# Low parts of the weights by an accumulating transfer onto the negated high part, in an encoder trunk with split fp32 products

## The chip, the cores and the metric

The kernel runs on one core of a Trainium2 chip. The metric is the device time of one execution in microseconds (us). Before the change the median of three runs is 3259.91 us (3259.77 to 3260.55).

## What is computed

An encoder trunk of four layers over 512 tokens with 16 learned meta tokens ahead, width 1024, fp32. The mixers of the layers are multi-head latent attention (MLA), differential attention, a bidirectional RG-LRU and MLA again; a SwiGLU feed-forward follows each, and every sub-layer has an RMS norm before and after it. Cut to the frame:

```python
def _swiglu(h, w_in, w_out):
    g, u = jnp.split(h @ w_in, 2, axis=-1)
    return (jax.nn.silu(g) * u) @ w_out
...
def _rglru_block(h, w_in, conv_w, conv_b, w_gates, b_gates, lam, w_o):
    xb, gate = jnp.split(h @ w_in, 2, axis=-1)
    xb = lax.conv_general_dilated(...) + conv_b
    y = (_rg_lru(xb, w_gates[0], ..., reverse=False)
         + _rg_lru(xb, w_gates[1], ..., reverse=True))
    return (y.astype(h.dtype) * jax.nn.gelu(gate)) @ w_o
```

The precision asked for is that of fp32, and TensorE multiplies a rounded form of it, fp32r. So every factor is split in two: `x = xh + xl` and `w = wh + wl`, where the high part is the value rounded to fp32r and the low part is the rest. A product is the sum of three: `wh*xh + wh*xl + wl*xh`.

## The kernel before

Activations are kept transposed, features on the 128 partitions and 528 positions (512 tokens, 16 meta) along the free axis, which a matmul covers in two spans, 272 and 256 wide. The program is eight stages in a row, mixer and feed-forward of each layer, with a `boundary` between two stages (residual, norm, the split of the new `x`, and the first matmuls of the next stage). The order of every instruction on every engine is the order in which the code is written.

All weights lie in HBM in the order of use as 456 chunks of 128 partitions: 344 of 1024 columns, 80 of 768, 16 of 640 and 16 of 512. The class `Weights` hands them out:

- `fetch` (L241) starts a chunk's load into a staging tile `ws` on the queue of SyncE (SP). There are two staging tiles, so a load waits until the split of the chunk two before has read its tile.
- `ensure` (L252) splits chunks in order up to a wanted number. For each, ScalarE (ACT) copies `ws` to `wh` with rounding (L261), and the engine named in `l_engine` subtracts, `wl = ws - wh` (L262). There are four buffers for `wh` and four for `wl`. VectorE (DVE) subtracts 280 chunks, in the feed-forward stages above all, and GpSimd (POOL) 176, in the mixers and the boundaries; `run`, `boundary` and `final` set `l_engine`.
- `next` (L267) hands out the next chunk and first asks `ensure` for the two chunks behind it, so the split of a chunk stands in each engine's order about two chunks ahead of its use. The number that `ensure` may reach is capped by `low`, the oldest chunk still in use, plus the number of buffers.

`mm3` (L340) issues the three products through `mm` (L327). `split_from` (L336) splits an activation: ACT casts the high part and DVE subtracts. In the RG-LRU stage the names are: `t` and `xc` are the convolution's steps on DVE, `xsh` and `xsl` the split of its result, `g` a gate, `th` and `gt` steps of the recurrence, which runs as a scan on DVE (L1532). In MLA a head's query is split into `qh` and `ql`, and its rotary part into `qsa` and `qsb`.

At the start `run` (L1600s) starts the loads of the first three chunks between those of `x`; at the end of the first boundary ACT copies a finished PSUM tile to SBUF (`t<-pa`, L607), which frees the PSUM tile for the next stage.

Of the kernel before, what the change touches and what calls it, by code (L numbers as in the profile page):

```python
# [18 lines left out]
F32 = mybir.dt.float32  # L19
# [6 lines left out]
P = 128  # L26
# [202 lines left out]

class Weights:  # L230

    BUFS = 4

    def __init__(self, k, dram, widths):
        self.k, self.dram, self.widths = k, dram, widths
        self.offs = np.concatenate([[0], np.cumsum(np.array(widths) * P)]).tolist()
        self.n_dma = self.n_split = self.use = self.low = 0
        self.stage, self.parts = {}, {}
        self.l_engine = k.nc.vector

    def fetch(self, upto):  # L241
        while self.n_dma < min(upto + 1, len(self.widths)):
            j = self.n_dma
            n = self.widths[j]
            t = self.k.wpool.tile([P, 1024], F32, name="ws", tag="ws", bufs=2)
            self.k.nc.sync.dma_start(
                out=t[:, 0:n],
                in_=self.dram[self.offs[j]:self.offs[j] + P * n].rearrange("(p n) -> p n", p=P))
            self.stage[j] = t
            self.n_dma += 1  # L250

    def ensure(self, upto):  # L252
        upto = min(upto, self.low + self.BUFS - 1, len(self.widths) - 1)
        while self.n_split <= upto:
            j = self.n_split
            self.fetch(j)
            n = self.widths[j]
            s = self.stage.pop(j)
            wh = self.k.wpool.tile([P, 1024], F32R, name="wh", tag="wh", bufs=self.BUFS)
            wl = self.k.wpool.tile([P, 1024], F32R, name="wl", tag="wl", bufs=self.BUFS)  # L260
            self.k.nc.scalar.copy(out=wh[:, 0:n], in_=s[:, 0:n])  # L261
            self.l_engine.tensor_tensor(out=wl[:, 0:n], in0=s[:, 0:n], in1=f32(wh[:, 0:n]), op=ALU.subtract)  # L262
            self.parts[j] = (wh, wl)
            self.n_split += 1
            self.fetch(j + 2)

    def next(self, hold=False, ahead=2):  # L267
        j = self.use
# [11 lines left out]
class Trunk:  # L280
# [218 lines left out]
    def boundary(self, tail, g1, g2, t0, first=False, last=False, after=None):  # L499

        ha, hb = halves(t0)
        (a0, a1), (b0, b1) = ha, hb
        W = self.W
        todo = [(k, half) for half in (ha, hb) for k in range(NK)]
        running = []

        def adv(n):

            for _ in range(n):
                if todo:
                    k, half = todo.pop(0)
                    running.append([3, self.residual(k, half[0], half[1], g2, first, last)])
                for r in reversed(running):
                    r[0] -= 1
                    next(r[1])
                running[:] = [r for r in running if r[0]]

        def ens(n):  # L520
            if not last:
                W.ensure(W.use + n)

        W.l_engine = self.nc.gpsimd
        if first:
            W.low = W.use
            W.l_engine = self.nc.vector
            ens(0)
            adv(4)
            ens(1)  # L530
            for k in (2, 4, 6):
                self.load_x(k, 1)
            adv(2)
        else:
            stat = {}

            def mid():
                self.tt(self.acc[:, a0:a1], self.acc[:, a0:a1], stat["sq"], ALU.add)
                st = self.stat([self.acc[:, a0:a1]])
                self.rstd(st, self.rpost[:, a0:a1], 1.0 / D)  # L540

            def done():
                W.retire(1)
                ens(3)

            for n, m in enumerate(tail.ms):
                ps = self.ps1()[:, 0:a1 - a0]
                tail(m, ps, a0, a1)
                stat["sq"] = self.evict_u(m, ps, a0, a1, g1, tail.add)
            ens(3)  # L550
            for n, m in enumerate(tail.ms):
                ps = (self.ps1() if n or len(tail.ms) == 1 else self.ps2())[:, 0:b1 - b0]
                early = m == 7 and len(tail.ms) == 2
                tail(m, ps, b0, b1, None if n else mid, (lambda: (adv(3), done())) if early else done)
                adv({5: 1, 6: 2}.get(m, 0) if len(tail.ms) > 2 else 3 * (m == 7 and not early))
                stat["sq"] = self.evict_u(m, ps, b0, b1, g1, tail.add)
            done()
            adv(3)
        parts = {}
        tiles = [] if last else [self.ps2() for _ in range(3)]  # L560

        def group(ks, half):
            if last:
                return
            for k in ks:
                if k // 2 not in parts:
                    parts[k // 2] = W.next(hold=True, ahead=0)
            self.group_half(tiles, parts, ks, *half, col0(t0))

        group(range(2), ha)  # L570
        if last:
            st = self.stat([self.acc[:, b0:b1], stat["sq"]])
            adv(1)
            self.rstd(st, self.rpost[:, b0:b1], 1.0 / D)
            adv(12)
            return None
        if not first:
            st = self.stat([self.acc[:, b0:b1], stat["sq"]])
            rest = self.rstd(st, self.rpost[:, b0:b1], 1.0 / D, late=True)
        if first:  # L580
            ens(1)
        group(range(2, 4), ha)
        adv(2)
        if not first:
            rest()
        ens(0)
        ens(1)
        W.l_engine = self.nc.gpsimd
        adv(2)
        sq = self.sq  # L590
        group(range(4, 8), ha)
        adv(2)
        group(range(0, 2), hb)
        self.tt(self.acc2[:, a0:a1], self.acc2[:, a0:a1], sq, ALU.add, None)
        sa = self.stat([self.acc2[:, a0:a1]])
        rest = self.rstd(sa, self.r[:, a0:a1], 1.0 / D, late=True)
        adv(2)
        group(range(2, 4), hb)
        W.retire(2)
        adv(4)  # L600
        rest()
        W.l_engine = self.nc.vector
        ens(0)
        group(range(4, 8), hb)
        W.retire(2)
        t = self.tmp()
        self.nc.scalar.copy(out=t[:, t0:NT], in_=tiles[0][:, col0(t0) + t0:col0(t0) + NT])  # L607
        tiles[0] = Shifted(t, col0(t0))
        sb = self.stat([self.acc2[:, b0:b1], self.sq])
        self.rstd(sb, self.r[:, b0:b1], 1.0 / D)  # L610
        if after is not None:
            self.load_table(after)
        ens(1)
        return tiles
# [19 lines left out]
    def final(self, get_chunks, kt, g1, t0, split, add=False):  # L634
# [3 lines left out]
        rng = spans(t0)  # L638
        W = self.W
        self.load_table(RSQRT)  # L640
        W.l_engine = self.nc.vector
        lead0 = W.use - len(self.led)
        for m in range(8 - split):
            if m in self.led:
# [14 lines left out]
                W.ensure(W.use + 1)  # L659
            self.evict_u(m, ps[:, col0(t0) + t0:col0(t0) + NT], t0, NT, g1, add)  # L660
        held, first = {}, self.W.use
        W.l_engine = self.nc.gpsimd
        for m in range(8 - split, 8):
            n = self.W.use
            self.W.low = max(self.W.low, min(self.W.use, first))
# [942 lines left out]
    def run(self):  # L1608
        nc, tc = self.nc, self.tc
        make_identity(nc, self.ident)  # L1610
        nc.vector.memset(self.ones, 1.0)
        nc.vector.memset(self.eps, EPS)
        self.load_table(RSQRT)
        nc.scalar.dma_start(out=self.sm[:, 0:S_MLA], in_=self.aps["small"][:, 0:S_MLA])
        for n in range(3):
            self.W.fetch(n)
            self.load_x(2 * n, 0)
        self.load_x(6, 0)
        self.load_x(0, 1)
        nc.scalar.dma_start(out=self.sm[:, S_MLA:S_N], in_=self.aps["small"][:, S_MLA:S_N])  # L1620
        tail, g1 = None, None
        for s in range(STAGES + 1):
            i = s // 2
            g2 = (lambda k, i=i, w=(2 if s % 2 else 0): self.gain(i, w, k)) if s < STAGES else None
            late = s >= 7 or s == STAGES
            t0 = NMETA if late else 0
            after = AF.Silu if s % 2 else (AF.Sigmoid if s == 4 else None)
            tiles = self.boundary(tail, g1, g2, t0, first=(s == 0), last=(s == STAGES), after=after)
            self.close_phase()
            if s == STAGES:  # L1630
                break
            self.open_phase()
            self.W.l_engine = nc.vector if s % 2 else nc.gpsimd
            if s % 2:
                tail, g1 = self.ffn(tiles, i, t0)
            elif s == 2:
                tail, g1 = self.diff(tiles, i)
            elif s == 4:
                tail, g1 = self.lru(tiles, i)
            else:  # L1640
                tail, g1 = self.mla(tiles, i, i // 3, NMETA if s == 6 else 0)
# [34 lines left out]
```

## Time and profile before

| | |
|---|---|
| median of three runs | 3259.91 us |
| the profiled execution | 3257.35 us |
| its span | 3255.3 us |
| granted TensorE clock, mean | 0.979 |
| TensorE (PE) busy | 3065.2 us, 94% |
| VectorE (DVE) busy | 1882.9 us, 58% |
| ScalarE (ACT) busy | 1395.9 us, 43% |
| GpSimd (POOL) busy | 752.7 us, 23% |
| read from HBM | 225.34 MB, 70 GB/s over the span |

The span is the time between the first and the last instruction of the profiled execution; some 2 us of its own time lie outside it. Busy shares are means over stages with different limits, so they are read together with the windows by stage. A wait is put down to the work that came last before it ended. A row of the timeline stands for neighbouring instructions of one kind; its duration is from the first one's start to the last one's end.

### The profile page before, as it was taken

How to read it: one execution, taken by the hardware profiler on the slowest of the kernel's cores; microseconds unless marked ns; L12 is line 12 of the kernel's file. 1: busy time of each engine (PE TensorE's matmuls, PEld its weight loads, DVE VectorE, ACT ScalarE, POOL GpSimd, SP SyncE). 2: the span in 40 equal slices, each digit the busy share in tenths (PEclk: the TensorE clock that was granted, in tenths of full speed). 3: DMA queues.
4: the chain of work that ended last, by engine and by line, in shares of the span. 5: the costliest groups of instructions: out<-in, count | busy, mean ns of one | idle time of the engine just before them, and what ended most of it. 6: DMA issues, size and time to landing. Idle time of an engine off the chain costs nothing. (4 is left out here: it accounts for less than half of the span.)

```text
span 3255.3 us, 53413 instructions
## 1 busy us (share of the span) xinstructions
PE 3065.2 (94%) x22384; PEld 2892.2 (89%) x22384; DVE 1882.9 (58%) x3003; ACT 1395.9 (43%) x2464; POOL 752.7 (23%) x514
## 2 busy tenths in 40 slices
PE   8999999999989998999988889999998999999998
PEld 7898898999979888999977889999987888888887
DVE  7766747443277767443278874544248676574433
ACT  5554544222256565222246553322235554442232
POOL 3232222000145523000045543000033322330001
PEclk9999999999999999999998999999999999999999
DMA  3011112222211112222221212222221111122222
GB/s 102 31 45 48 37 46 78 90 91 92 90 62 40 56 37 72 91 91 93 88 67 59 67 58 90 91 91 89 95 65 55 47 37 48 53 77 96 97 97 80
DMA packets 71600, 230.88 MB, mean 71 GB/s; under 512 B 7824, under 2 KB 12304, under 8 KB 71360
## 3 DMA queue, kind: packets, MB, share of 16 engines
q1 hardware_dynamic: 70144, 225.54, 21.5%
q8 instruction: 176, 2.88, 0.4%
q10 hardware_dynamic: 1216, 1.93, 0.2%
q14 instruction: 64, 0.52, 0.0%
HBM read 225.34 MB, written 2.10 MB: 70 GB/s over the span
## 5 line engine op out<-in xcount | busy, mean ns | idle before, releaser
L327 PE MATMUL pa<-xh,wh 128*128 128x272 f32 (+2 forms) x4120 | 955.0, 303 | 18.3 <-ACT xh L318 7.5
L327 PE MATMUL pa<-xh,wl 128*128 128x272 f32 (+2 forms) x3776 | 891.3, 299 | 3.5 <-POOL wl L262 3.5
L327 PE MATMUL pa<-xl,wh 128*128 128x272 f32 (+1 forms) x3776 | 809.8, 288 | 43.9 <-DVE xl L324 43.2
L327 PEld LDWEIGHTS pa<-xl,wh 128*128 128x128 f32 x3776 | 620.2, 190 | 88.9 <-DVE xl L324 59.3
L327 PEld LDWEIGHTS pa<-xh,wh 128*128 128x128 f32 x4120 | 665.0, 190 | 34.9 <-DVE ql L324 9.1
L262 DVE TENSOR_TENSOR wl<-ws,wh 128x1024 fp32r<-128x1024 f32 (+1 forms) x280 | 330.6, 1183 | 510.3 <-ACT wh L261 510.3
L327 PEld LDWEIGHTS pa<-xh,wl 128*128 128x128 f32 x3776 | 615.6, 190 | 8.6 <-POOL wl L262 3.9
L262 POOL TENSOR_TENSOR wl<-ws,wh 128x1024 fp32r<-128x1024 f32 (+3 forms) x176 | 388.8, 2215 | 725.6 <-ACT wh L261 665.8
L321 POOL TENSOR_TENSOR acc<-acc,t 128x256 f32<-128x256 f32 (+3 forms) x158 | 164.2, 1040 | 1528.2 <-ACT t L318 1523.9
L261 ACT CAST wh<-ws 128x1024 fp32r<-128x1024 f32 (+3 forms) x456 | 440.6, 980 | 160.2 <-DMA ws<-in_w 142.9
L321 DVE TENSOR_TENSOR t<-pa,r 128x528 f32<-128x528 f32 (+1 forms) x193 | 135.5, 703 | 277.5 <-PE pa L327 277.4
L327 PE MATMUL pa<-hh,wl 128*128 128x272 f32 (+2 forms) x1078 | 249.6, 301 | 0.0
L327 PE MATMUL pa<-hl,wh 128*128 128x272 f32 (+2 forms) x1078 | 248.5, 300 | 0.0
L327 PE MATMUL pa<-hh,wh 128*128 128x272 f32 (+2 forms) x1078 | 246.6, 299 | 0.0
L337 ACT CAST hh<-t 128x528 fp32r<-128x528 f32 (+1 forms) x88 | 55.4, 630 | 400.0 <-DVE t L321 400.0
L793 ACT CAST pth<-pa 128x528 fp32r<-128x528 f32 (+3 forms) x200 | 118.7, 593 | 236.7 <-PE pa L782 234.8
L318 ACT ACTIVATE t<-t 128x528 f32<-128x528 f32 (+3 forms) x121 | 72.2, 597 | 294.0 <-DVE t L321 292.7
L327 PEld LDWEIGHTS pa<-hh,wh 128*128 128x128 f32 x1078 | 171.3, 189 | 6.4
L327 PEld LDWEIGHTS pa<-hh,wl 128*128 128x128 f32 x1078 | 171.2, 189 | 6.2
L327 PEld LDWEIGHTS pa<-hl,wh 128*128 128x128 f32 x1078 | 169.2, 188 | 7.4
L321 DVE TENSOR_TENSOR ptl<-pa,pth 128x528 fp32r<-128x528 f32 (+1 forms) x160 | 111.6, 698 | 73.7 <-ACT pth L793 69.2
L782 PE MATMUL pa<-ident,p 128*128 128x128 f32 (+3 forms) x840 | 139.3, 281 | 2.7 <-DVE p L769 2.6
(286 smaller groups left out, 5220.9 us busy)
## 6 DMA issues: line engine op xcount, KB each, us to landing
ws<-in_w SPq DMA_DIRECT2D x344, 512.0 KB, 3.4
ws<-in_w SPq DMA_DIRECT2D x80, 384.0 KB, 3.3
ws<-in_w SPq DMA_DIRECT2D x16, 320.0 KB, 2.9
ws<-in_w SPq DMA_DIRECT2D x16, 256.0 KB, 2.7
out<-h SPq DMA_DIRECT2D x16, 128.0 KB, 1.7
h<-in_x SPq DMA_DIRECT2D x4, 272.0 KB, 3.9
h<-in_x SPq DMA_DIRECT2D x4, 256.0 KB, 4.1
cos<-in_tab ACTq DMA_DIRECT2D x2, 264.0 KB, 4.3
```

Source lines behind the costliest of these rows:

```text
L261: self.k.nc.scalar.copy(out=wh[:, 0:n], in_=s[:, 0:n])
L262: self.l_engine.tensor_tensor(out=wl[:, 0:n], in0=s[:, 0:n], in1=f32(wh[:, 0:n]), op=ALU.subtract)
L318: return self.nc.scalar.activation(out=out, in_=in_, func=func, **kw)
L321: return (eng or self.nc.vector).tensor_tensor(out=out, in0=a, in1=b, op=op)
L327: self.nc.tensor.matmul(out, lhsT=lhsT, rhs=rhs, start=start, stop=stop)
L337: self.nc.scalar.copy(out=oh, in_=src)
L782: self.nc.tensor.transpose(ps[0:kb - ka, c0 + qa:c0 + qb], ptiles[qt][0:qb - qa, ka:kb], self.ident[0:qb - qa, 0:qb - qa])
L793: self.nc.scalar.copy(out=hi[0:n, w], in_=src)
```

## The change

Four things change in `Weights`, and the places that set the engine follow.

1. `wl` no longer comes from the staging tile. The engine named in `negate` writes `wl = -wh` (DVE by a multiplication with -1 for 386 chunks; ACT by an activation for 66 chunks, in the RG-LRU stage and in part of the boundaries and `final`). Then POOL issues a transfer of the same chunk from HBM that adds what it brings onto `wl`, which leaves `w - wh` there. There are 452 such transfers; each chunk is so read from HBM twice. The first four chunks (`DIRECT`) keep the subtraction, on DVE.
2. `wh` and `wl` have six buffers each instead of four.
3. There is one staging tile instead of two. It is free again when ACT has copied it (for the first four chunks, when DVE has subtracted too), and only then does the next load start.
4. `ensure` looks two chunks further ahead (`EXTRA`), under the cap of six buffers.

At the start only the first chunk's load stands ahead of the loads of `x`, and the scratch for transfers that POOL issues is halved.

```diff
-    BUFS = 4
+    BUFS = 6
+    EXTRA = 2
+    DIRECT = 4
...
-            t = self.k.wpool.tile([P, 1024], F32, name="ws", tag="ws", bufs=2)
...
+            t = self.k.wpool.tile([P, 1024], F32, name="ws", tag="ws", bufs=1)
+            self.k.nc.sync.dma_start(out=t[:, 0:n], in_=self.chunk(j))
...
-        upto = min(upto, self.low + self.BUFS - 1, len(self.widths) - 1)
+        upto = min(upto + (self.EXTRA if upto >= self.DIRECT else 0), self.low + self.BUFS - 1, len(self.widths) - 1)
...
             self.k.nc.scalar.copy(out=wh[:, 0:n], in_=s[:, 0:n])
-            self.l_engine.tensor_tensor(out=wl[:, 0:n], in0=s[:, 0:n], in1=f32(wh[:, 0:n]), op=ALU.subtract)
+            if j < self.DIRECT:
+                self.k.tt(wl[:, 0:n], s[:, 0:n], f32(wh[:, 0:n]), ALU.subtract)
...
+                self.fetch(j + 1)
+                continue
+            if self.negate is self.k.nc.scalar:
+                self.k.act(wl[:, 0:n], f32(wh[:, 0:n]), AF.Copy, scale=-1.0)
+            else:
+                self.negate.tensor_scalar(out=wl[:, 0:n], in0=f32(wh[:, 0:n]), scalar1=-1.0, scalar2=None,
+                                          op0=ALU.mult)
+            self.k.nc.gpsimd.dma_start(out=wl[:, 0:n], in_=self.chunk(j), accum_op=ALU.add)
             self.parts[j] = (wh, wl)
             self.n_split += 1
-            self.fetch(j + 2)
+            self.fetch(j + 1)
...
@@ boundary
-        W.l_engine = self.nc.gpsimd
+        W.negate = self.nc.scalar
         if first:
             W.low = W.use
-            W.l_engine = self.nc.vector
+            W.negate = self.nc.vector
...
@@ final
         held, first = {}, self.W.use
-        W.l_engine = self.nc.gpsimd
+        W.negate = self.nc.scalar
...
@@ run
+        self.W.fetch(0)
         for n in range(3):
-            self.W.fetch(n)
             self.load_x(2 * n, 0)
...
-            self.W.l_engine = nc.vector if s % 2 else nc.gpsimd
+            self.W.negate = nc.scalar if s == 4 else nc.vector
...
-    nc = bacc.Bacc("TRN2", target_bir_lowering=False, num_devices=1, dynamic_dma_scratch_size=4096)
+    nc = bacc.Bacc("TRN2", target_bir_lowering=False, num_devices=1, dynamic_dma_scratch_size=2048)
```

The lines behind `ensure` move down: ACT's copy of a chunk is L261 before and L266 now, the helper of activations L318 and L334, the cast of `split_from` L337 and L353, additions and products L321 and L337, and L278 is the accumulating transfer. Below, each row is an instruction's line, operation and tiles; a number behind a tile's name tells buffers of one name apart, and xN is N such instructions in a row.

ACT at the end of the first boundary, around the copy that frees a PSUM tile, before:

```order
L318 ACTIVATE xh<-h,sm 128x256
L318 ACTIVATE t<-h 128x256 x2
L261 CAST wh<-ws 128x1024
L607 COPY t<-pa 128x528
L318 ACTIVATE r<-pb,eps 128x256
L261 CAST wh<-ws 128x1024
```

and now:

```order
L334 ACTIVATE xh<-h,sm 128x256
L334 ACTIVATE t<-h 128x256 x2
L266 CAST wh<-ws 128x1024 x3
L623 COPY t<-pa 128x528
L334 ACTIVATE r<-pb,eps 128x256
L266 CAST wh<-ws 128x1024
```

Three chunks' copies stand ahead of the PSUM tile's copy, where one stood.

ACT in the RG-LRU stage, from the roots of one pair of blocks (`th`) over the cast of the next block's input (`xsh`) to its gates (`g`), before:

```order
L261 CAST wh<-ws 128x1024
L318 ACTIVATE th_18841<-th_18841 128x528
L318 ACTIVATE th_18864<-th_18864 128x528
L318 ACT_TABLE_LOAD
L318 ACTIVATE junk<-eps 128x1
L337 CAST xsh_19010<-xc_18445 128x528
L337 CAST xsh_19026<-xc_18798 128x528
L261 CAST wh<-ws 128x1024 x2
L318 ACTIVATE g<-pa,sm 128x528 x4
```

and now:

```order
L266 CAST wh<-ws 128x1024
L334 ACTIVATE wl<-wh 128x1024
L334 ACTIVATE th_19081<-th_19081 128x528
L334 ACTIVATE th_19104<-th_19104 128x528
L334 ACT_TABLE_LOAD
L334 ACTIVATE junk<-eps 128x1
L353 CAST xsh_19252<-xc_18679 128x528
L353 CAST xsh_19268<-xc_19037 128x528
L266 CAST wh<-ws 128x1024
L334 ACTIVATE wl<-wh 128x1024
L266 CAST wh<-ws 128x1024
L334 ACTIVATE wl<-wh 128x1024
```

Each copy of a chunk has its negation behind it on the same engine; one pair stands ahead of `th` and two ahead of the gates, and the copies are where they were.

POOL in the RG-LRU stage, over one round of blocks, before:

```order
L321 TENSOR_TENSOR g<-g,xc_19461 128x528
L262 TENSOR_TENSOR wl<-ws,wh 128x1024 x3
L321 TENSOR_TENSOR xc_19137<-th_19931,th_19933 128x528
L321 TENSOR_TENSOR xc_19461<-th_19951,th_19953 128x528
L262 TENSOR_TENSOR wl<-ws,wh 128x1024 x2
```

and now:

```order
L337 TENSOR_TENSOR g<-g,xc_19709 128x528
L278 DMA wl<-in_w 128x1024 x3
L337 TENSOR_TENSOR xc_19381<-th_20186,th_20188 128x528
L337 TENSOR_TENSOR xc_19709<-th_20206,th_20208 128x528
L278 DMA wl<-in_w 128x1024 x2
```

Where POOL subtracted five chunks in a round it now issues five transfers, at the same places among its other work.

## Rows read from the trace of the kernel before

**Rows 1.** The page's first part: busy us, share of the span and instructions of each engine.

```profile
PE 3065.2 (94%) x22384; PEld 2892.2 (89%) x22384; DVE 1882.9 (58%) x3003; ACT 1395.9 (43%) x2464; POOL 752.7 (23%) x514
```

**Rows 2.** Windows by stage: the first MLA, the first feed-forward, the differential attention, the RG-LRU. Columns: window, its length, busy us (and instructions) of PE, PE's weight loads, DVE, ACT, POOL, then the granted clock as a share of full speed, the DMA engines' busy share, GB/s.

```profile
45.00:480.00 435.00, 412.48 (x3197) 384.27 (x3198) 301.40 (x646) 225.45 (x465) 116.13 (x67) 0.98 0.13 41
530.00:890.00 360.00, 360.00 (x2950) 359.92 (x2949) 136.86 (x152) 99.26 (x134) 13.64 (x9) 1.00 0.28 90
...
930.00:1240.00 310.00, 288.17 (x2154) 271.10 (x2155) 213.35 (x433) 193.18 (x379) 143.54 (x106) 0.96 0.14 47
1680.00:1945.00 265.00, 215.58 (x1559) 210.17 (x1557) 221.83 (x198) 150.62 (x209) 138.66 (x69) 0.90 0.20 64
```

**Rows 3.** The list of PE's waits: what PE's matmuls waited for, us in total, times, the longest.

```profile
PE pa L327 <- DVE xl L324: 43.2, 58, 2.4
PE pa L327 <- DVE ql L324: 29.9, 16, 2.6
PE pa L327 <- DVE gt L321: 19.4, 6, 3.7
PE pa L327 <- DVE t L321: 13.9, 6, 3.9
PE pa L327 <- ACT xsh L337: 9.6, 2, 6.0
...
PE pa L327 <- POOL wl L262: 5.4, 3, 2.9
```

**Rows 4.** Timeline of DVE in the RG-LRU stage: start us, duration us, engine, line, operation, tiles, xcount.

```profile
1695.42 4.39 DVE L324 SCALAR_TENSOR_TENSOR xc<-t,sm,xc 128x526 f32<-128x526 f32 x3
...
1701.30 2.37 DVE L324 SCALAR_TENSOR_TENSOR xc<-t,sm,xc 128x526 f32<-128x526 f32 x3
...
1715.82 0.71 DVE L324 SCALAR_TENSOR_TENSOR th<-t,th 128x528 f32<-128x528 f32 x1
...
1717.18 2.78 DVE L324 SCALAR_TENSOR_TENSOR th<-t,th 128x528 f32<-128x528 f32 x1
...
1754.60 2.85 DVE L321 TENSOR_TENSOR t<-g 128x528 f32<-128x528 f32 x1
```

**Rows 5.** Timeline of POOL, ACT and PE in the same stage; in brackets the idle time before the row and what ended it.

```profile
1690.20 0.41 PE L327 MATMUL pa<-xsl,wh 128*128 128x272 f32 x2
...
1696.90 2.35 POOL L262 TENSOR_TENSOR wl<-ws,wh 128x1024 fp32r<-128x1024 f32 x1 [3.35 <-ACT wh L261]
...
1700.48 0.81 PE L327 MATMUL pa<-xsh,wh 128*128 128x272 f32 x2 [3.88 <-DVE t L321]
1701.09 0.64 PE L327 MATMUL pa<-xsl,wh 128*128 128x272 f32 x2
...
1716.49 2.91 POOL L262 TENSOR_TENSOR wl<-ws,wh 128x1024 fp32r<-128x1024 f32 x1 [4.61 <-ACT wh L261]
...
1754.46 2.43 POOL L262 TENSOR_TENSOR wl<-ws,wh 128x1024 fp32r<-128x1024 f32 x1 [5.19 <-issue]
...
1758.23 0.64 ACT L318 ACTIVATE th<-th 128x528 f32<-128x528 f32 x1 [2.87 <-DVE th L324]
```

**Rows 6.** The page's queue, group and transfer rows for the weights. A queue's row: packets, MB, its packets' time as a share of 16 engines' span. A group's row: instructions, busy us, mean ns of one, idle us before them and what ended most of it. A transfer's row: count, KB each, median us from issue to landing.

```profile
q1 hardware_dynamic: 70144, 225.54, 21.5%
...
L262 DVE TENSOR_TENSOR wl<-ws,wh 128x1024 fp32r<-128x1024 f32 (+1 forms) x280 | 330.6, 1183 | 510.3 <-ACT wh L261 510.3
...
L261 ACT CAST wh<-ws 128x1024 fp32r<-128x1024 f32 (+3 forms) x456 | 440.6, 980 | 160.2 <-DMA ws<-in_w 142.9
...
ws<-in_w SPq DMA_DIRECT2D x344, 512.0 KB, 3.4
ws<-in_w SPq DMA_DIRECT2D x80, 384.0 KB, 3.3
...
ws<-in_w SPq DMA_DIRECT2D x16, 256.0 KB, 2.7
```

**Rows 7.** Timeline of ACT, DVE and PE at the begin of a head in the first MLA stage, columns as in rows 5.

```profile
97.17 1.66 ACT L261 CAST wh<-ws 128x640 fp32r<-128x640 f32 x2
...
97.78 0.49 DVE L769 TENSOR_SCALAR p<-p,st 128x528 f32<-128x528 f32 x1
...
100.03 2.77 DVE L321 TENSOR_TENSOR qsa<-t,qsa 64x528 fp32r<-64x528 f32 x1
...
104.42 0.41 PE L327 MATMUL pa<-kh,qh 128*16 128x272 f32 x2 [2.56 <-DVE ql L324]
```

**Rows 8.** Timeline of ACT and DVE at the program's start, columns as in rows 5.

```profile
3.90 0.83 ACT L261 CAST wh<-ws 128x768 fp32r<-128x768 f32 x1 [1.67 <-DMA ws<-in_w]
...
13.35 0.83 ACT L261 CAST wh<-ws 128x768 fp32r<-128x768 f32 x1 [0.67 <-DMA ws<-in_w]
...
14.38 0.95 DVE L262 TENSOR_TENSOR wl<-ws,wh 128x768 fp32r<-128x768 f32 x1
...
25.58 1.04 ACT L261 CAST wh<-ws 128x1024 fp32r<-128x1024 f32 x1
...
27.65 0.60 ACT L607 COPY t<-pa 128x528 f32<-128x528 f32 x1 [1.03 <-PE pa L327]
```

**Rows 9.** Timeline of DVE at the boundary behind the first feed-forward stage.

```profile
890.69 0.43 DVE L321 TENSOR_TENSOR h<-h,t 128x272 f32<-128x272 f32 x1
891.04 2.06 DVE L321 TENSOR_TENSOR t<-u,rpost 128x272 f32<-128x272 f32 x1
```

More of the change, by code (lines that the diff above doesn't have):

```diff
@@ L238, in __init__, with chunk @@
         self.stage, self.parts = {}, {}
-        self.l_engine = k.nc.vector
+        self.negate = k.nc.vector
+    def chunk(self, j):
+        n = self.widths[j]
+        return self.dram[self.offs[j]:self.offs[j] + P * n].rearrange("(p n) -> p n", p=P)
     def fetch(self, upto):
@@ L244, in fetch @@
             n = self.widths[j]
-            t = self.k.wpool.tile([P, 1024], F32, name="ws", tag="ws", bufs=2)
-            self.k.nc.sync.dma_start(
-                out=t[:, 0:n],
-                in_=self.dram[self.offs[j]:self.offs[j] + P * n].rearrange("(p n) -> p n", p=P))
+            t = self.k.wpool.tile([P, 1024], F32, name="ws", tag="ws", bufs=1)
+            self.k.nc.sync.dma_start(out=t[:, 0:n], in_=self.chunk(j))
             self.stage[j] = t
@@ L261, in ensure @@
             self.k.nc.scalar.copy(out=wh[:, 0:n], in_=s[:, 0:n])
-            self.l_engine.tensor_tensor(out=wl[:, 0:n], in0=s[:, 0:n], in1=f32(wh[:, 0:n]), op=ALU.subtract)
+            if j < self.DIRECT:
+                self.k.tt(wl[:, 0:n], s[:, 0:n], f32(wh[:, 0:n]), ALU.subtract)
+                self.parts[j] = (wh, wl)
+                self.n_split += 1
+                self.fetch(j + 1)
[6 more added lines that the diff above has]
+            self.k.nc.gpsimd.dma_start(out=wl[:, 0:n], in_=self.chunk(j), accum_op=ALU.add)
             self.parts[j] = (wh, wl)
             self.n_split += 1
-            self.fetch(j + 2)
+            self.fetch(j + 1)
     def next(self, hold=False, ahead=2):
@@ L601, in boundary @@
         rest()
-        W.l_engine = self.nc.vector
+        W.negate = self.nc.vector
         ens(0)
@@ L640, in final @@
         self.load_table(RSQRT)
-        W.l_engine = self.nc.vector
+        W.negate = self.nc.vector
         lead0 = W.use - len(self.led)
@@ L661, in final @@
         held, first = {}, self.W.use
-        W.l_engine = self.nc.gpsimd
+        W.negate = self.nc.scalar
         for m in range(8 - split, 8):
```

## The prediction

> **What bounds the kernel now.** I began with the share of busy time: TensorE (PE) is busy 3065.2 us, 94% of the profiled span [rows 1]. That is a mean over stages, so the windows by stage come next [rows 2]. In the first feed-forward stage (530 to 890 us) PE is busy 360.00 of 360 us: nothing done to other engines can shorten it, and the other three feed-forward stages are built the same. In the RG-LRU stage (1680 to 1945 us) PE is busy 215.58 of 265 us, so 49.4 us are idle, and the granted clock is 0.90 on average. The first attention stage (MLA) leaves 22.5 us and the differential attention 21.8 us. Those three, the start and the seams between the stages are where a change to the weight path can act.
>
> What ends PE's idle time is in the list of PE's waits [rows 3]. It is hardly ever the weights: the low part `wl` ends three waits, 5.4 us in all. It is VectorE (DVE): `xl` 43.2 us, `ql` 29.9, `gt` 19.4, `t` 13.9, and `xsh`, which ScalarE (ACT) makes, 9.6. The last three with `wl` make 48.3 us, nearly the RG-LRU stage's 49.4 us; `gt`, `t` and `xsh` exist in that stage alone. So the change pays if it makes DVE faster there, not if it makes weights earlier.
>
> **Why DVE is late there.** In the RG-LRU stage GpSimd (POOL) subtracts `wl`. The timeline shows three additions in a row (`xc`) in 2.37 us at 1701.30 with no subtraction beside them, and the same three in 4.39 us at 1695.42 with one; a single `th` takes 0.71 us alone and 2.78 us beside the subtraction at 1716.49 [rows 4, 5]. Each meeting costs DVE about 2.0 us. PE pays: the wait for `t` at 1700.48 is 3.88 us, behind the delayed additions, and the wait for `xsh` stands behind the 2.85 us `t` of 1754.60, which held ACT for 2.87 us [rows 5].
>
> **The change, part by part.** The sum is made against the profiled execution, 3257.35 us, which is 2.6 us below the median of 3259.91.
>
> *Feed-forward stages.* Per chunk DVE trades a subtraction of 1.18 us [rows 6] for a negation. Its price is not in the trace at this size: at least the 0.49 us of a scaling of 528 elements [rows 7], at most the subtraction. I take 0.95, the 528 row scaled up, since it is the same operation. DVE is idle most of the time there (136.86 of 360 us busy), so this is worth 0. The added transfers double the weights' share of the DMA engines, 21.5% over the span [rows 6], to 43% if an accumulating transfer occupies them as long as a plain one. A whole chunk feeds 48 matmuls, 5.9 us of PE (360 us for 2950 of them [rows 2]). 1.5 us of engine time per load (21.5% of the span over 456 chunks), twice, fits in that; and so does the cycle of the single staging tile, load 3.4 and copy 1.04, 4.4 us with nothing between [rows 6, 8]. So **0**; the other bound is a rival.
>
> *RG-LRU stage.* The subtractions leave POOL; ACT makes the negations there, at about the 1.04 us of its copy [rows 8], and POOL only issues transfers. The 12 waits for `gt` and `t` (33.3 us) each hold one meeting of about 2.0 us: -24. ACT's negations lie ahead of about nine of them, in the order shown above the rows: +9. The `xsh` waits shrink from 9.6 to about 2.2, since the copy and negation behind them come after the casts: -7.4. The three `wl` waits at the stage's end go from 5.4 to about 1: -4. That is -26. The clock: a mean of 0.90 over 265 us is, between the full level and the half (2.4 and 1.2 GHz), about 53 us at half. The fall follows long idle: after the 3.88 us wait the pairs of matmuls take 0.81 and 0.64 us where 0.41 is usual [rows 5]. 53 us at half cost 26.5 us; half of the idle time gone should give back about half, I take -12. Sum **-38**. Bounds: 0, if nothing is unblocked; -62, if all idle time goes and half of the lost clock returns.
>
> *Start.* With one staging tile the first four chunks, whose subtraction still reads it, go one behind the other: load 3.3, copy 0.83, subtraction 0.95, together 5.1 us, and the fourth copy starts at 3.90 + 3 x 5.1 = 19.1 instead of 13.35 [rows 6, 8]: +5.8. Later ACT is given three copies in a row ahead of the copy `t<-pa`, which frees a PSUM tile, where there was one (the order at the start). Each of the two more waits for its load: 2 x (3.4 + 1.04) = 8.9 us. `t<-pa` so comes 14 us after its 27.65, at about 41.5, and PE has nothing in between but what its other tiles hold. I take **+14**, the clock's part included. Bounds: +9 (PE has work under the first serial loads) to +17 (a slow clock after the gap).
>
> *Seams.* At each of seven boundaries POOL's subtraction delays DVE once or more (2.06 us for an addition of 0.43 [rows 9]), which goes; but ACT waits for the single tile and negates ahead of the first `xh`, some 2.5 us. Net +0.4 each: **+3**, bounds -7 to +13.
>
> *MLA, twice.* At a head's begin DVE's `qsa` takes 2.77 us beside POOL's subtraction [rows 7], and PE then waits 2.56 us for `ql`. That delay goes. But ACT splits two chunks there in 1.66 us, both loaded ahead; with one tile the second copy waits for a load that starts when the first copy ends, 2.7 to 3.3 us, with `qh` queued behind it. A wait on a weight takes the place of one on a subtraction: 0 to +0.5 per head. The stages' beginnings gain about 2.5 us each. Sum **-1**, bounds -30 to +15.
>
> *Differential attention.* The same exchange: **+1**, bounds -5 to +9.
>
> *Look-ahead.* Six buffers and two more chunks: by the instruction order nearly every chunk has at least 72 matmuls between its split and its use, 10 us and more, against 3.4 us for a load; the accumulation should land in time.
>
> Sum: -38 + 14 + 3 - 1 + 1 = **-21**; 3259.9 - 21 = **3239 us**.
>
> **A rule weighed against the rows.** The rows show POOL's subtraction and DVE's two-input operations shutting each other out. What POOL's issue of a transfer does beside DVE no row shows. The Trainium skill, "SBUF — State Buffer", section "Who interferes with whom", says that a DVE instruction with two SBUF inputs collides with a GpSimd instruction that reads SBUF, not with one that only writes, but that DVE operations in a two-port mode, such as scalings, shut out GpSimd entirely, and that GpSimd cannot write the descriptors of its own transfers meanwhile. By the first half the RG-LRU gain is whole, as in my sum; by the second the negations on DVE in MLA delay the accumulations, which the look-ahead covers at 1 us or so each.
>
> **Rivals.**
> *POOL's issue blocks as the subtraction did.* If issuing holds POOL and DVE for about 2 us per chunk, the RG-LRU gain goes and the costs stay: -21 + 38 = +17, 3277 us. At half that hold it is -2, 3258 us, no change. For it: in this kernel whatever POOL does with SBUF beside DVE has cost about 2 us. Against: an issue moves no tile through POOL. The section named above says that whichever begins first holds the pair for its whole instruction; its price here would be the 2.0 us of the rows.
>
> *The single staging tile becomes the wait* (the other side). Loads and accumulations share the DMA engines; in a load that shares, 3.4 us become more. In the order I count about 41 places outside feed-forward where ACT must split a second chunk right behind a first with work for PE queued behind. At 4.5 us a load, each loses 1.1 us: +45, 3284 us. It decides once the mean load passes about 3.9 us (+21, all of the gain). From about 4.8 us on the tile's cycle no longer fits in the 5.9 us of a feed-forward chunk either. For it: ACT already waits 142.9 us for `ws` [rows 6] with two tiles. Against: the engines are idle for most of the time in these stages (share 0.13 to 0.20 [rows 2]).
>
> *More is gained.* If loads land earlier than the median says, the second copies wait little, and MLA and differential attention keep their gain: `ql` 29.9 and part of `xl`, some -34 more: 3205 us.
>
> *The accumulation is slow.* If it occupies the DMA engines three times as long as a load, 4.5 us and more, the two no longer fit in 5.9 us; some 60 chunks in each of four stages at +0.6 us each give +144, about 3400. Unlikely: the engines' share is 0.28 there [rows 2].
>
> **How the numbers follow.** My forecast 42%; more gained 15%; the issue blocks half 13%, and fully 5%; the single tile 20%; slow accumulation 5%. About 0.2% (6.5 us) is what a measurement here can tell from no change. Faster 0.57, same 0.13, slower 0.30. The range reaches from 10 us below the larger gain to 6 above the single tile: 3195 to 3290; only the slow accumulation and the far bounds lie outside.
>
> **What would show it.** In the changed profile: PE idle in the RG-LRU stage down from 49 to some 25 us and its clock up from 0.90; `xc` triples at 2.4 us throughout; a PE wait near 34 to 41 us behind three copies; ACT's wait for `ws` far above 142.9 us; `ql` waits about as now; PE's waits for `wl` staying small. I am wrong if DVE operations in the RG-LRU stage stay long beside POOL's issues, if feed-forward is no longer full, or if PE waits for `wl` in many places.

## The result and the profile after

The changed kernel takes 3289.18 us, median of four runs (3287.26 to 3290.95), against 3259.91: 1.0089 times the time before, 95% interval 1.0072 to 1.0107. It is slower by 29 us, where 21 us less were forecast. The profiled execution has a span of 3286.8 us (3255.3 before).

PE executes the same 22384 matmuls in either trace, so the start of one and the same matmul marks the same place in the program. The table gives the time between such marks, cut where the windows of before were cut, and in brackets PE's idle time. The last two columns are two of the experiments below. Idle time is counted from the first matmul on, and the last row ends with the last one; the 0.5 us that are missing to the 31.5 between the spans lie behind it and in rounding.

| stage (us of before) | before | forecast | change | two tiles, 5 buffers (ws2_5) | all subtraction on DVE (b_dve_5_1) |
|---|---|---|---|---|---|
| start, 0-45 | 46.0 (2.7) | +14 | +17.5 (13.0) | +10.6 (10.1) | +3.3 (3.5) |
| first MLA, 45-480 | 434.1 (21.5) | -0.5 | +5.4 (24.2) | -17.9 (8.3) | -15.0 (11.5) |
| differential attention, 930-1240 | 308.9 (20.6) | +1 | +13.4 (28.1) | -16.1 (13.3) | -4.9 (19.7) |
| RG-LRU, 1680-1945 | 265.1 (49.4) | -38 | -37.4 (23.1) | -55.7 (12.6) | -31.8 (27.8) |
| its output projection and seam, 1945-2050 | 104.9 (6.4) | +0.4 | +13.7 (14.2) | +12.8 (14.5) | +3.1 (7.9) |
| second MLA, 2450-2845 | 395.0 (26.8) | -0.5 | +8.9 (31.0) | -16.9 (14.2) | -14.0 (18.8) |
| three feed-forward windows | 1080.1 (0.0) | 0 | 0.0 (0.0) | 0.0 (0.0) | 0.0 (0.0) |
| the other six seams | 256.2 (45.2) | +2.6 | +8.6 (46.0) | -1.7 (40.1) | +16.2 (54.7) |
| end, 2890-3255 | 352.7 (0.1) | 0 | +0.9 (0.1) | +2.0 (1.0) | -0.1 (0.1) |

The RG-LRU stage gained what was forecast. The losses lie in MLA, in the differential attention, behind the RG-LRU and at the start. Length less idle time is the time that PE is busy with the same matmuls, and it grew as well: by 24.0 us over the whole span, where the idle time grew by 7.5. The first part of the page, columns as in [rows 1]:

```profile
PE 3089.2 (94%) x22384; PEld 2911.6 (89%) x22384; DVE 1638.0 (50%) x3113; ACT 1468.5 (45%) x2530; POOL 751.2 (23%) x790
```

The windows of the changed kernel for the first feed-forward, the differential attention, the RG-LRU and the stretch behind it, columns as in [rows 2]:

```profile
554.10:914.10 360.00, 360.00 (x2950) 359.92 (x2949) 103.92 (x155) 103.17 (x136) 64.38 (x71) 1.00 0.83 181
956.80:1279.10 322.30, 294.18 (x2154) 276.55 (x2155) 215.34 (x459) 195.08 (x380) 97.60 (x104) 0.94 0.40 90
1721.70:1949.40 227.70, 204.62 (x1560) 200.86 (x1559) 157.45 (x190) 178.12 (x237) 77.02 (x67) 0.95 0.65 143
1949.40:2068.00 118.60, 104.39 (x766) 99.58 (x765) 46.94 (x89) 57.66 (x105) 39.65 (x42) 0.94 0.72 153
```

Feed-forward is full as before although the DMA engines are now 83% busy there. In the RG-LRU window the granted clock rose from 0.90 to 0.95 as PE's idle time fell; DVE needs 157 us instead of 222 [rows 2]. What that stage's DVE rows look like now:

```profile
1732.20 2.37 DVE L340 SCALAR_TENSOR_TENSOR xc<-t,sm,xc 128x526 f32<-128x526 f32 x3
...
1735.82 2.38 DVE L340 SCALAR_TENSOR_TENSOR xc<-t,sm,xc 128x526 f32<-128x526 f32 x3
```

with POOL's issue of a transfer beside the second:

```profile
1735.70 0.86 POOL L278 DMA_DIRECT2D wl<-in_w  x1 [4.86 <-ACT wl L334]
```

These three additions take 2.37 to 2.38 us, as they did alone [rows 4]; the 4.39 us beside a subtraction are gone, and POOL's issue does not replace them. It is not so throughout: of the 36 additions `xc` 24 were slow before (1.68 to 2.79 us, where 0.77 is usual) and 7 still are. Each of the seven overlaps one of POOL's own sums `xc` or products `g`, which the change leaves where they were; the worst three in a row:

```profile
1772.68 8.54 DVE L340 SCALAR_TENSOR_TENSOR xc<-t,sm,xc 128x526 f32<-128x526 f32 x3
```

PE's waits now, columns as in [rows 3]:

```profile
PE pa L343 <- DVE ql L340: 24.7, 11, 4.1
PE pa L343 <- ACT xh L334: 22.1, 10, 5.5
PE pa L343 <- DVE pth L337: 13.9, 7, 3.6
PE pa L343 <- ACT g L334: 12.1, 5, 3.8
PE pa L343 <- ACT xh L353: 11.2, 5, 3.6
PE pa L343 <- ACT t L623: 9.7, 1, 9.7
...
PE pa L343 <- DVE t L337: 4.4, 4, 1.7
PE pa L343 <- ACT xsh L353: 3.7, 1, 3.7
...
PE pa L343 <- DVE gt L337: 3.3, 2, 2.6
```

`t`, `gt` and `xsh` fell from 42.9 to 11.4 us. In their place stand waits for what ACT makes, or DVE from it: `xh`, `pth`, `g`, the PSUM copy `t`. ACT's own waits say why; and the page has the transfers (queue, group and transfer rows, columns as in [rows 6]):

```profile
ACT wh L266 <- DMA ws<-in_w: 555.3, 206, 6.9
```

```profile
q0 software_dynamic: 65088, 219.71, 41.4%
q1 hardware_dynamic: 70144, 225.54, 20.7%
...
L278 POOL DMA_DIRECT2D wl<-in_w x452 | 393.5, 871 | 2177.5 <-DVE wl L276 1421.3
...
ws<-in_w SPq DMA_DIRECT2D x344, 512.0 KB, 3.5
wl<-in_w POOLq DMA_DIRECT2D x344, 512.0 KB, 5.9
```

ACT waits 555.3 us for the staging tile instead of 142.9 [rows 6], yet a load still lands in 3.5 us in the median (the mean of all is 3.7 where it was 3.4, the longest 6.9): loads became little slower, they start late. Some 313 of the 555 us lie in the feed-forward stages, where PE stays full; outside them the wait went from 39 to 243 us. The start shows it:

```profile
19.52 0.83 ACT L266 CAST wh<-ws 128x768 fp32r<-128x768 f32 x1 [2.31 <-DMA ws<-in_w]
...
31.62 1.04 ACT L266 CAST wh<-ws 128x1024 fp32r<-128x1024 f32 x1
35.97 1.04 ACT L266 CAST wh<-ws 128x1024 fp32r<-128x1024 f32 x1 [3.31 <-DMA ws<-in_w]
43.30 1.04 ACT L266 CAST wh<-ws 128x1024 fp32r<-128x1024 f32 x1 [6.29 <-DMA ws<-in_w]
44.25 0.59 ACT L623 COPY t<-pa 128x528 f32<-128x528 f32 x1
```

```profile
44.89 0.81 PE L343 MATMUL pa<-xh,wh 128*128 128x272 f32 x2 [9.72 <-ACT t L623]
```

Three copies, two waits for the tile, then the PSUM copy at 44.25 instead of 27.65 [rows 8], and PE idle for 9.72 us. In the differential attention the same happens ahead of `pth`, which the list of PE's waits of before did not have among its larger entries:

```profile
983.52 1.03 ACT L266 CAST wh<-ws 128x1024 fp32r<-128x1024 f32 x1
988.05 1.05 ACT L266 CAST wh<-ws 128x1024 fp32r<-128x1024 f32 x1 [3.50 <-DMA ws<-in_w]
989.00 0.58 ACT L809 CAST pth<-pa 32x528 fp32r<-32x528 f32 x1
```

```profile
990.61 0.39 PE L343 MATMUL pa<-fold,p 48*128 48x16 f32 x2 [1.76 <-DVE pth L337]
```

Before, the same matmul began without a wait. And at the begin of a head in MLA, with two copies ahead of `qsa` and `qh`:

```profile
265.24 0.60 ACT L266 CAST wh<-ws 128x512 fp32r<-128x512 f32 x1
269.19 1.04 ACT L266 CAST wh<-ws 128x1024 fp32r<-128x1024 f32 x1 [3.34 <-DMA ws<-in_w]
270.14 0.63 ACT L947 CAST qsa<-t 64x528 fp32r<-64x528 f32 x1
```

```profile
273.31 0.40 PE L343 MATMUL pa<-kh,qh 128*16 128x272 f32 x2 [3.38 <-ACT xh L353]
```

Before, the same matmul waited 2.56 us for `ql`, like that of an earlier head in [rows 7].

### The profile page after: what moved, and what is told of

Same layout as the page of the kernel before. It is cut to its first block, busy times and chain, and to the rows that moved or that the text cites. A ratio compares the mean times of both kernels' runs of the same rounds, so it can differ in the third digit from the quotient of the medians.

```text
span 3286.8 us, 54325 instructions
## 1 busy us (share of the span) xinstructions
PE 3089.2 (94%) x22384; PEld 2911.6 (89%) x22384; DVE 1638.0 (50%) x3113; ACT 1468.5 (45%) x2530; POOL 751.2 (23%) x790
## 3 DMA queue, kind: packets, MB, share of 16 engines
q0 software_dynamic: 65088, 219.71, 41.4%
q1 hardware_dynamic: 70144, 225.54, 20.7%
## 5 line engine op out<-in xcount | busy, mean ns | idle before, releaser
L343 PE MATMUL pa<-xh,wh 128*128 128x272 f32 (+2 forms) x4120 | 961.6, 305 | 44.1 <-ACT xh L334 22.1
L278 POOL DMA_DIRECT2D wl<-in_w x452 | 393.5, 871 | 2177.5 <-DVE wl L276 1421.3
L266 ACT CAST wh<-ws 128x1024 fp32r<-128x1024 f32 (+3 forms) x456 | 447.0, 980 | 561.4 <-DMA ws<-in_w 555.3
L276 DVE TENSOR_SCALAR wl<-wh 128x1024 fp32r<-128x1024 f32 (+3 forms) x386 | 255.3, 662 | 795.8 <-ACT wh L266 795.4
L337 DVE TENSOR_TENSOR t<-pa,r 128x528 f32<-128x528 f32 (+1 forms) x193 | 135.4, 702 | 295.6 <-PE pa L343 295.4
L353 ACT CAST hh<-t 128x528 fp32r<-128x528 f32 (+1 forms) x88 | 55.5, 630 | 355.7 <-DVE t L337 355.7
L337 POOL TENSOR_TENSOR acc<-acc,t 128x256 f32<-128x256 f32 (+3 forms) x158 | 167.6, 1061 | 156.1 <-ACT t L334 153.4
L334 ACT ACTIVATE t<-t 128x528 f32<-128x528 f32 (+3 forms) x121 | 72.1, 596 | 269.5 <-DVE t L337 269.5
L337 DVE TENSOR_TENSOR ptl<-pa,pth 128x528 fp32r<-128x528 f32 (+1 forms) x160 | 111.7, 698 | 66.6 <-ACT pth L809 62.1
```

What stands on the lines that cost most here:

```text
L276: self.negate.tensor_scalar(out=wl[:, 0:n], in0=f32(wh[:, 0:n]), scalar1=-1.0, scalar2=None, op0=ALU.mult)
L278: self.k.nc.gpsimd.dma_start(out=wl[:, 0:n], in_=self.chunk(j), accum_op=ALU.add)
L334: return self.nc.scalar.activation(out=out, in_=in_, func=func, **kw)
L337: return (eng or self.nc.vector).tensor_tensor(out=out, in0=a, in1=b, op=op)
L343: self.nc.tensor.matmul(out, lhsT=lhsT, rhs=rhs, start=start, stop=stop)
L353: self.nc.scalar.copy(out=oh, in_=src)
```

## The experiments

The theory after these rows, T: the single staging tile makes the loss, by ACT's waits in the order of its instructions, and the accumulation itself makes the gain. Rivals: the longer look-ahead does it, by longer bursts of copies (V); the doubled traffic or POOL's issues do it (U). Each of the eleven kernels was timed beside the kernel before; behind its time stand the ratio to that and the 95% interval.

**Two staging tiles, four buffers, no extra look-ahead (ws2_4).**

```diff
-    BUFS = 6
-    EXTRA = 2
+    BUFS = 4
+    EXTRA = 0
-  name="ws", tag="ws", bufs=1)
+  name="ws", tag="ws", bufs=2)
-            self.fetch(j + 1)
+            self.fetch(j + 2)
```

The loads at the start are also in the order of before.

> The accumulation alone: two staging tiles, four buffers and the look-ahead of before, and the loads at the start in the order of before. If the single tile causes the loss (T): the RG-LRU keeps its 37 us and the 68 us lost elsewhere go, 3222; up to 20 less if MLA and differential attention gain too. If the extra look-ahead's bursts of copies on ACT cause it (V): the same 3222. If the doubled traffic or POOL's issue of transfers causes it (U): it stays near 3285.

3303.32 us, 1.0136 (1.0121 to 1.0151). No theory foresaw it. PE's waits of this kernel:

```profile
PE pa L343 <- DMA wl<-in_w: 106.3, 39, 8.0
```

One of them in the timelines of POOL and PE: after two negations in a row on DVE (the second begins at 188.56) POOL issues twice, and PE is 4.53 us late:

```profile
189.38 1.79 POOL L278 DMA_DIRECT2D wl<-in_w  x2 [9.74 <-DVE wl L276]
```

```profile
195.44 0.51 PE L343 MATMUL pa<-xh,wl 128*128 128x272 f32 x2 [4.53 <-DMA wl<-in_w]
```

A low part is ready only after copy, negation, issue and a transfer of about 6 us, where the subtraction took 1.2 us on DVE [rows 6] and 2.3 to 2.9 on POOL [rows 5]. With the look-ahead of before that is late, even in feed-forward (+6.5 us and more in each of its windows). So the look-ahead is what the accumulation needs (ws2_5 below has 14.0 of the 106.3 us left); U as stated is not it, since the RG-LRU stage keeps its gain here (-44.1 us).

**One tile, four buffers, no extra look-ahead (ws1_4).** As ws2_4, but with the change's single tile and its loads.

> The change with four buffers and no extra look-ahead, but one staging tile. T: the loss stays or grows, 3285 to 3310. V: it falls to 3225 to 3250. U: 3289, as the change.

3369.54 us, 1.0340 (1.0324 to 1.0355). Both costs together: PE waits 83.2 us on `pa` for accumulations, and ACT 465.4 us for the tile. V falls in its simple form. Against ws2_4 the single tile, with the order of the first loads, costs 66 us.

**The kernel before with one staging tile (b_ws1).**

```diff
-  name="ws", tag="ws", bufs=2)
+  name="ws", tag="ws", bufs=1)
-            self.fetch(j + 2)
+            self.fetch(j + 1)
```

> The kernel before with one staging tile and nothing else; the subtraction, which still reads the tile, holds it 1 to 2.5 us longer than in the change. T: slower than before by 68 us or more, 3325 to 3400. U or V: at most 20 us slower.

3554.28 us, 1.0906 (1.0888 to 1.0925): +295, beyond what T said. ACT waits 1113.6 us for the tile. The subtraction holds the tile too here, so this prices one tile without accumulation. It is 185 us slower than ws1_4, with the same tile, buffers and look-ahead; how much of that is the subtraction's hold on the tile, and how much POOL's subtraction beside DVE, no run separates.

**Two tiles, five buffers, one chunk of extra look-ahead (ws2_5).** As ws2_4 with `BUFS = 5` and `EXTRA = 1`; six buffers beside two tiles do not fit in SBUF.

> The change with two staging tiles, paid for by five buffers instead of six and one chunk of extra look-ahead instead of two, loads at the start in the order of before. T: as ws2_4 within 5 us, 3215 to 3227. V: half the loss stays, about 3255. U: 3285.

3173.38 us, 0.9735 (0.9718 to 0.9751), 42 us below even T's low end. The same head of MLA now, ACT and then PE:

```profile
248.68 1.55 ACT L266 CAST wh<-ws 128x1024 fp32r<-128x1024 f32 x2
250.13 0.63 ACT L947 CAST qsa<-t 64x528 fp32r<-64x528 f32 x1
```

```profile
253.67 0.40 PE L343 MATMUL pa<-kh,qh 128*16 128x272 f32 x2 [0.30 <-DVE ql L340]
```

Both copies run without a wait, and PE's wait is 0.30 us. By the table MLA and the differential attention gain 51 us against the kernel before, where the change lost 28, and the RG-LRU gains 18 more than in the change.

**The change with five buffers and one chunk of look-ahead (ws1_5).**

```diff
-    BUFS = 6
-    EXTRA = 2
+    BUFS = 5
+    EXTRA = 1
```

> The change with five buffers and one chunk of extra look-ahead, so that it differs from ws2_5 (3173) by the second staging tile and the order of the first loads alone. If the single tile costs what ws2_5 suggests: 3289 or more, since the change with one more buffer has 3289; I expect 3310 to 3340. If the sixth buffer and the second chunk of look-ahead had been what hurt: 3180 to 3250.

3274.22 us, 1.0038 (1.0025 to 1.0052). Against ws2_5 the second tile (with the order of the first loads) is worth 101 us; the start holds 4 of the 93 us between the two profiled spans. It is also 15 us faster than the change itself, which none of the two expectations held: a sixth buffer and a second chunk of look-ahead together cost 15.

**More look-ahead without accumulation (b_5_1).** The kernel before with five buffers and one chunk of extra look-ahead.

```diff
-    BUFS = 4
+    BUFS = 5
+    EXTRA = 1
-        upto = min(upto, self.low + ...
+        upto = min(upto + (self.EXTRA if upto >= 4 else 0), self.low + ...
```

> The kernel before, with subtraction on DVE and POOL as before, but five buffers and one chunk of extra look-ahead (two staging tiles, as before). If look-ahead only repays what the accumulation's late landing costs: 3245 to 3265. If look-ahead itself is the gain of ws2_5: about 3175 to 3200.

3258.43 us, 0.9998 (0.9989 to 1.0008). Look-ahead alone is worth nothing here.

**All subtractions on DVE (b_dve_5_1).** b_5_1 with `l_engine` set to DVE everywhere.

> As b_5_1, but every subtraction on DVE, none on POOL. If the gain is POOL's subtractions gone, whatever replaces them: 3170 to 3185. If DVE's time counts as well (a subtraction holds it 1.22 us where a negation holds it 0.66, and 1.22 more at each of the 176 chunks that POOL had): 3200 to 3240.

3213.96 us, 0.9858 (0.9842 to 0.9875). As the second expectation had it: the subtractions moved from POOL to DVE are worth 44 us against b_5_1, without any accumulation; the table's last column has most of it in the RG-LRU and MLA. The other 41 us up to ws2_5 come with the negation and accumulation, above all in the RG-LRU (24), the seams (18) and the differential attention (11), against a loss behind the RG-LRU and at the start.

**The two places where ws2_5 still loses (fix).**

```diff
-    DIRECT = 4
+    DIRECT = 8
...
-            if j < self.DIRECT:
+            if j < self.DIRECT or j in self.lru_out:
```

`lru_out` are the 16 chunks of the RG-LRU's output projection.

> ws2_5 with the first eight chunks subtracted on DVE instead of four, and also the 16 chunks of the RG-LRU's output projection, the two places where ws2_5 still loses against before (10.6 and 12.8 us). If PE waits there for late accumulations: 3150 to 3160. If something else is late there: 3168 to 3175.

3158.77 us, 0.9688 (0.9673 to 0.9702). The start goes from +10.6 to +1.1 us, the projection and its seam from +12.8 to +5.7; there PE's three waits for accumulations, 8.0 us in ws2_5, are gone. In ws2_5 the reason was, at the start,

```profile
39.51 0.81 PE L343 MATMUL pa<-xh,wl 128*128 128x272 f32 x2 [8.35 <-DMA wl<-in_w]
```

PE's wait for an accumulation issued at 30.19, whose chunk is used too soon.

**Six buffers, one tile, one chunk of look-ahead (ex1).** The change with `EXTRA = 1`.

> The change (one staging tile, six buffers) with one chunk of extra look-ahead instead of two. ws1_5, which has five buffers as well, took 3274. If the second chunk of look-ahead makes the 15 us between it and the change (longer bursts of copies on ACT, each waiting for the one tile): 3270 to 3278. If the sixth buffer makes it: 3289.

3389.28 us, 1.0396 (1.0378 to 1.0413): both expectations wrong by over 100 us. The loss is in MLA (+53.9 and +58.7 us against before). ACT there, and PE behind it:

```profile
285.41 1.04 ACT L266 CAST wh<-ws 128x1024 fp32r<-128x1024 f32 x1
289.12 0.62 ACT L266 CAST wh<-ws 128x512 fp32r<-128x512 f32 x1 [2.68 <-DMA ws<-in_w]
295.48 1.04 ACT L266 CAST wh<-ws 128x1024 fp32r<-128x1024 f32 x1 [5.73 <-DMA ws<-in_w]
296.43 0.63 ACT L947 CAST qsa<-t 64x528 fp32r<-64x528 f32 x1
```

```profile
299.60 0.60 PE L343 MATMUL pa<-kh,qh 128*16 128x272 f32 x2 [9.50 <-ACT xh L353]
```

The limits on `ensure` decide which chunks are split at one place. Here three copies fall ahead of `qsa`, with two waits for the tile, where the change has two copies and one wait. PE's wait is 9.50 instead of 3.38 us. This is the cost of a single tile in its plainest form: a burst of k copies makes k - 1 waits for a whole load, in front of whatever stands next in ACT's order. So with one tile the sixth buffer alone costs 115 us (ws1_5 to ex1), and the second chunk of look-ahead gives 100 of them back in the change; which copies fall together was looked at for this one head.

**fix with three staging tiles (fix_ws3), and with subtraction on DVE inside feed-forward (fix_ffn).**

```diff
-  name="ws", tag="ws", bufs=2)
+  name="ws", tag="ws", bufs=3)
-            self.fetch(j + 2)
+            self.fetch(j + 3)
```

> fix (3159) with three staging tiles. ACT still waits 68 us for loads in fix. If those waits are off the critical path, as the list of PE's waits says: 3154 to 3162. If staging still limits: 3130 to 3150.

3158.18 us, 0.9685 (0.9670 to 0.9699): no difference to fix. Two tiles are enough.

```diff
-            if j < self.DIRECT or j in self.lru_out:
+            if j < self.DIRECT or j in self.lru_out or self.sub:
```

`sub` is set while the code of a feed-forward stage is written.

> fix (3159) with subtraction on DVE instead of negation and accumulation for every chunk split inside the four feed-forward stages, which takes more than half of the extra traffic away. If the accumulation is worth nothing where PE is full, and its traffic costs nothing there: 3155 to 3163. If the doubled traffic costs time there: 3130 to 3150. If DVE's longer subtraction hurts: over 3165.

3158.79 us, 0.9689 (0.9675 to 0.9704): no difference either. Where PE is full the accumulation neither gains nor costs.

## Why the prediction was wrong

The forecast was -21 us and the change made +31 in the profiled spans. Of the 52 us between them, MLA holds 15, the projection and seam behind the RG-LRU 13, the differential attention 12, the other seams 6, the start 3.5 and the rest 2. Split another way by the same table, some 24 of the 52 lie in PE's idle time (the start counted whole) and some 28 in slower matmuls.

**What held.** Feed-forward 0: exact. The RG-LRU: -38 forecast, -37.4 measured, 26.3 of it idle time (forecast 26) and 11 the clock (forecast 12, 0.90 to 0.95). That POOL's subtraction against DVE's operations was the cost, and not the weights' arrival, b_dve_5_1 shows from the other side. But that the sum came out so close is in part luck. In this stage the waits for `gt` and `t` were 10, 29.9 us, and not 12: two of the six `t` waits lie in MLA, so `t` does not exist in the RG-LRU alone. They fell by the 24 us forecast. The +9 put down to ACT's negations came as 11 us of waits for `g`, and the tile makes those: a copy ahead of the gates waits for it, ws1_5 has the same 12.1 us of them, and ws2_5, where ACT negates as well, has 0.3. A wait for the tile was not in this stage's sum at all. The start: +14 forecast, +17.5 measured; the second of the two loads took ACT 6.29 us of waiting instead of 3.4, beside the first accumulations.

**The first step that failed** is the exchange: "A wait on a weight takes the place of one on a subtraction: 0 to +0.5 per head." I let the new wait cancel a gain place by place, so MLA and the differential attention both came out near nothing. In MLA the exchange came out at the upper end, +0.5 us of PE's idle time at the seven later heads of the first stage and +0.6 in the second, while the gain of 2.5 us put at each stage's beginning was 1.7 in one and nothing in the other. In the differential attention there was little to exchange: six of the seven waits for `pth`, 13.5 us, stand where PE had not waited, and the waits behind DVE that went (`sd` and `vl`) are 7.7. Its +13.4 lies outside the bounds given (+9), and so do the seven seams together, with the output projection, +22.3 against +13. What the two sides are worth by themselves the experiments show: with two tiles these three stages gain 51 us (ws2_5), with one they lose 12 (ws1_5) or 28 (the change), so the tile costs 63 us there, all else but the order of the first loads equal, and 79 lie between ws2_5 and the change. The wait stands wherever two copies meet in ACT's order, also where no subtraction had delayed anything, as ahead of `pth`. And its price is a whole load with everything behind it on ACT.

Behind the RG-LRU, which I had counted as one seam of +0.4, the chunks are 768 columns wide, and PE needs one in 4.4 us (36 matmuls at 360 us for 2950), while copies follow each other in the changed kernel at

```profile
2001.87 0.84 ACT L266 CAST wh<-ws 128x768 fp32r<-128x768 f32 x1 [2.04 <-DMA ws<-in_w]
2006.60 0.84 ACT L266 CAST wh<-ws 128x768 fp32r<-128x768 f32 x1 [3.90 <-DMA ws<-in_w]
2010.89 0.83 ACT L266 CAST wh<-ws 128x768 fp32r<-128x768 f32 x1 [2.20 <-DMA ws<-in_w]
```

4.3 to 4.7 us: the tile's cycle is as long as the work it feeds. I had tested that cycle for the wide chunks of feed-forward alone. The tile is the smaller part of this stretch all the same: ws1_5 loses 17.1 us there and ws2_5, with two tiles, 12.8, to late accumulations in the main; what remains in fix (+5.7) was not traced further.

**The second step that failed** is the clock, which the forecast priced in the RG-LRU and at the start and put at nothing elsewhere, without a reason. Length less idle time in the table says what it cost: the same matmuls took 7.4 us longer in the two MLA stages, 5.9 in the differential attention, 5.9 behind the RG-LRU and 7.8 in the other seams. The mean granted clock fell from 0.979 to 0.972 (in the differential attention from 0.96 to 0.94), which between 2.4 and 1.2 GHz is some 137 and 184 us at the lower level. The lower level stands for the most part behind waits, the new ones now, as in the RG-LRU before. One microsecond behind the wait of 1.76 us shown above a pair of matmuls takes 0.81 us, where 0.40 is usual:

```profile
991.81 0.81 PE L343 MATMUL pa<-ks,qs 128*128 128x272 f32 x2 [0.22 <-DVE sd L1281]
```

**The rivals.** The single tile as the bound was put at 3284 us, and 3289 was measured. Its place and sign were right, its mechanism was not, and that the numbers meet is luck: I had it work through loads stretched to 4.5 us by the traffic, and the median load is 3.5, the mean 3.7. POOL's issue as a blocker fell: of 39 operations on DVE with 528 elements and their inputs in SBUF that overlapped an issue in the changed kernel, the median is 0.71 us, as it is beside nothing. The slow accumulation half holds: it does occupy the engines longer than a load, twice as long and not three times, and feed-forward has room. Its price was wrong by its own numbers: 4.5 and 1.5 us exceed 5.9 by 0.1 and not 0.6, which makes 24 us and not 144. That more would be gained if the copies did not wait is what ws2_5 did.

**The rule.** The Trainium skill, "SBUF — State Buffer", section "Who interferes with whom", was cited for two things. The trace agrees with its first half: DVE's two-input operations run at full speed beside POOL's issues (0.71 us), and the seven slow `xc` of the changed kernel all meet operations of POOL that read tiles. Of the second, that DVE's two-port operations lock GpSimd out of writing descriptors, little shows here: in the view of that line by form, POOL's issue takes 0.847 us at least, 0.865 in the median and 1.152 at most (the three numbers in ns ahead of the comma):

```profile
L278 POOL DMA_DIRECT2D wl<-in_w x452: 847/865/1152, 34.7 to 3251.7; - x151
```

So any lock costs an issue 0.3 us at the most in its visible time here; and in fix, where 47 issues overlapped a scaling or negation on DVE, their median is 0.88 us and the longest 1.33, against 0.87 and 1.17 beside nothing on DVE. What it does to the transfer behind an issue no run separates.

**The look-ahead** was put at no cost and no gain, the accumulation landing in time. In the change it does, but for two waits of 2.8 us together behind the RG-LRU. But ws2_4 shows that this rests on the extra look-ahead, 130 us between it and ws2_5, which also has the fifth buffer, and ws1_5 and ex1 that with one tile the order of the copies matters as much: 3274 and 3389 us for one buffer's difference.

## What to carry to other kernels

When a buffer is taken away, walk through the in-order engine that reads it and count the bursts: k copies in a row cost k - 1 whole loads in front of whatever comes next, even where loads are short and the engine is half idle. Price a new wait by itself at each of its places, and a gain by itself, before letting one cancel the other; and add what PE's new waits do to its clock, here more than the waits themselves. A longer path to a ready operand (here copy, negation, issue, transfer) needs look-ahead of its own length, and the two changes are worth nothing apart: 3303 and 3258 us, together 3173.

## What the runs showed of the hardware

In the changed kernel an accumulating transfer costs the DMA engines twice a plain one: 41.4% of their span for 219.71 MB against 20.7% for 225.54 MB, 2.05 times per byte; one of 512 KB lands in 5.9 us in the median where the load takes 3.5. I had counted 43% for both queues together; they take 62%. POOL needs 0.87 us to issue one. A negation of 1024 elements takes DVE 0.69 us in the median (forecast 0.95) where the subtraction takes 1.23 in the kernel before.
